# Context weights stored 32 bytes further on in their tiles, in a two-layer mixer block on one core

## The chip, the cores and the metric

The kernel runs on one core of a Trainium2 chip. The metric is the device time of one execution in microseconds (us). TensorE (PE) does the matrix products and loads their weights (PEld in the profile), ScalarE (ACT) the activations, VectorE (DVE) elementwise work, GpSimd (POOL) a few powers, SyncE (SP) issues the transfers.

## The reference

A stream `x` of 512 tokens and a context of 256 tokens, both 1024 wide, go through two layers. In each, both are normalised and modulated, projected by one wide matrix, and mixed by four branches (retention, a short convolution, a 31-tap convolution, windowed attention); each branch is gated, and an output matrix brings the sum back. The second layer needs of the context only keys and values.

```
for l in range(DEPTH):                       # 2
    hx = modulate(rmsnorm(x, norm_w[l]), shift_x, scale_x)
    hc = modulate(rmsnorm(xc, norm_w[l]), shift_c, scale_c)
    px = split_proj(hx @ w_in[l])
    pc = split_proj(hc @ w_in[l])            # layer 1: ret_k, ret_v, att_k, att_v alone
    ...
    # mixer_output, for x and (in layer 0) for the context:
    merged = sum(sigmoid(g) * (br @ w_branch[i]) for i, (g, br) in enumerate(zip(gates, (r, s, f, a))))
    out = merged @ w_out
    x = x + gate_x * out_x
    xc = xc + gate_c * out_c
return rmsnorm(x, final_norm_w)
```

## The kernel before

Everything is held transposed, with 128 channels on the partitions and the tokens along the columns: 512 columns for the stream, 256 for the context. A weight of a projection (kind "a"), gate ("g") or output ("o") is a block of 1024 input channels by 128 output channels, held as [128, 1024], that is eight chunks of 128 x 128 side by side, 512 bytes each in a partition.

To keep float32 accuracy every operand is split into a high part and a low part, each of a type (float32r) that TensorE takes in one pass. `split` and `pair` do it for the data, `w_split` for the weights: ACT copies the raw weight into the high tile `wh`, DVE subtracts and writes the low tile `wl`. `mm3` then makes three products for each chunk: high weight x high data, high weight x low data, low weight x high data. So a weight has 8 x 3 = 24 products, all added up in one of three PSUM tiles `d`. For the context the high and low data of a chunk (256 columns each) lie in one row of 2048 bytes, one behind the other (`pair`, `Half`); for the stream each has a row of its own.

The weight tiles are three pairs (`self.wt`, `wh0`, `wl0`, `wh1`, ...), taken in turn by `take`. They are allocated one behind the other in one pool, and behind them lie the softmax tiles `p`, the constants `cst`, `vec` and small tables. A weight's key is (kind, layer, index, s), with s = 1 for the context and 0 for the stream; so `key[3]` is s. For s = 1 the raw weight comes in two rows of 512 columns and is split in two halves (208 in all), for s = 0 in one tile of 1024 columns. For kind "g" a second weight, that of the branch, is split into two rows (`wkeep`) and not into `wt`.

TensorE's order is that of the program. `w_get` hands out a weight and lets `w_ahead` split the next ones until two are ready. Beside the dense products run side flows (attention, retention, convolution taps, norms), which `slot` puts between the products by estimates of a planner (`Tally`).

The order of the run: `start` makes the context's norm and its first three projections chunk by chunk; its modulation products there use `s4`, a weight tile of 4 columns read at `s4[:, 2 * h + k]`, with h from 0 to 3 and k 0 or 1, four floats (16 bytes) apart. Then come the context's mixer (54 projections in all, 32 gates) and `mix_out` (8 outputs), the stream's mixer of layer 0, ten key and value projections of the context for layer 1, the stream's mixer of layer 1, and `final`, which makes the stream's last output in two halves of 256 columns.

Of the kernel before, what the change touches and what calls it, by code (L numbers as in the profile page):

```python
# [9 lines left out]
F32R = mybir.dt.float32r  # L10
# [15 lines left out]
P = 128  # L26
# [97 lines left out]
class Row:  # L124
# [3 lines left out]
    def __init__(self, free, ring, tile, w, parts):  # L128
        self.free, self.ring = free, ring
        self.r = tile[:, :w] if parts else None  # L130
        self.a = tile[:, :w].bitcast(F32) if parts else tile[:, :w]
# [146 lines left out]
class Block:  # L278
    def __init__(self, ctx, tc, xc, vec, cst, w_a, w_g, w_b, w_o, w_m, out):
        self.tc, self.nc = tc, Tally(tc.nc)  # L280
        self.xc, self.out = xc, out
        self.wsrc = {"a": w_a, "g": w_g, "b": w_b, "o": w_o}
        self.w_m = w_m

        rp = ctx.enter_context(tc.tile_pool(name="rp", bufs=1))
        rp.tile([P, PAD], F32, name="fill")
        self.arena = Arena(rp, NROWS, 12)
        self.arena.relief = self.relief

        self.cp = cp = ctx.enter_context(tc.tile_pool(name="cp", bufs=1))  # L290
        self.wraw = [cp.tile([P, 1024], F32, name=f"w{i}") for i in range(2)]
        self.wt = [[cp.tile([P, 1024], F32R, name=f"w{p}{i}") for p in "hl"] for i in range(3)]
        self.pt = [cp.tile([P, 640], F32, name=f"p{i}") for i in range(6)]
        pp = ctx.enter_context(tc.tile_pool(name="pp", bufs=1, space=PSUM))
        nc = self.nc
        self.cst = cp.tile([P, NC_], F32, name="cst")
        self.vec = cp.tile([P, NV], F32, name="vec")
        nc.sync.dma_start(self.vec, vec)
        nc.sync.dma_start(self.cst[:, :NCE], cst[:, :NCE])
        self.late_consts = lambda: nc.sync.dma_start(self.cst[:, NCE:], cst[:, NCE:])  # L300
        self.rings = {}
        self.dense = [pp.tile([P, 512], F32, name=f"d{i}") for i in range(3)]
        self.ovs = [pp.tile([P, 512], F32, name="ov")]
        self.work = [pp.tile([P, 512], F32, name=f"k{i}") for i in range(4)]
        self.turn = {}
        self.wq, self.wraws, self.wready, self.wkeep = [], [], {}, {}
        self.lanes = [[] for _ in range(5)]
        self.turns = 0
        self.flow = None
# [135 lines left out]
    def w_split(self):  # L445
        nc = self.nc
        key, raws = self.wraws.pop(0)
        parts = [self.take("wt")]
        for _, raw, o in raws:
            if o is None:  # L450
                hi, lo = self.part(), self.part()
                self.wkeep[key] = (hi, lo)
                hi, lo = hi.r, lo.r
                parts.append((hi, lo))
            else:
                hi, lo = (x[:, o] for x in parts[0])
            nc.scalar.activation(hi, raw, AF.Copy)
            nc.vector.tensor_tensor(lo, raw, hi.bitcast(F32), op=ALU.subtract)
        self.wready[key] = parts
# [1011 lines left out]
```

## Time and profile before

| | |
|---|---|
| median of 3 runs | 1831.67 us (1830.37 to 1833.78) |
| the profiled execution | 1832.62 us, of which the span from its first to its last instruction is 1830.5 us |
| mean granted clock of TensorE | 0.994 |
| PE, PEld, DVE, ACT busy | 98%, 85%, 73%, 46% of the span |

A time in the profile is that of one profiled execution. PE's busy time holds the recorded durations of matmuls, which overlap one another; how fast PE goes is seen from the distance between two starts (the pitch). A granted clock of 1.00 is 2.4 GHz.

### The profile page before, as it was taken

What the parts mean: (1) busy time and instruction counts of PE and PEld (TensorE: products, weight loads), DVE (VectorE), ACT (ScalarE), POOL (GpSimd) and SP (SyncE); (2) the same over time, 40 slices, a digit from 0 to 9 for tenths busy, and PEclk for the clock granted to TensorE, in tenths of its full rate; (3) what the DMA queues carried; (4) which work ended last, traced back from release to release, by engine and by line L of the source; (5) the groups of instructions that cost most, each with busy time, mean ns of one, the idle gap of its engine ahead of it and who ended that gap; (6) DMA issues with size and microseconds to landing.
All of it is one profiled execution on the core that took longest, in us unless ns stands there. A gap on an engine that the chain in (4) does not pass through costs nothing. (4 is left out here: it accounts for less than half of the span.)

```text
span 1830.5 us, 27546 instructions
## 1 busy us (share of the span) xinstructions
PE 1799.5 (98%) x10224; PEld 1562.1 (85%) x10224; DVE 1329.4 (73%) x2643; ACT 847.1 (46%) x1616; POOL 27.9 (2%) x34
## 2 busy tenths in 40 slices
PE   6999999999999999999999999999999999999997
PEld 4999999998888888788888889888888888888887
DVE  8899999884556669996898457447999865444445
ACT  6666765553554544423423336445534554323232
POOL 1000000000000000000000000000000000000000
PEclk8999999999999999999999999999999999999999
DMA  8736377743122222233555552322122222332233
GB/s 306 252 125 213 111 242 231 235 138 116 69 70 67 84 81 83 91 108 124 185 170 168 169 182 75 116 70 70 66 91 87 80 98 87 115 104 87 87 117 114
DMA packets 104646, 232.60 MB, mean 127 GB/s; under 512 B 12864, under 2 KB 20800, under 8 KB 104512
## 3 DMA queue, kind: packets, MB, share of 16 engines
q1 hardware_dynamic: 104512, 230.84, 37.9%
q8 instruction: 80, 1.31, 0.3%
q14 instruction: 54, 0.44, 0.1%
HBM read 218.73 MB, written 5.24 MB: 122 GB/s over the span
## 5 line engine op out<-in xcount | busy, mean ns | idle before, releaser
L187 PE MATMUL d<-r,wh 128*128 128x512 f32 (+1 forms) x3136 | 942.7, 383 | 0.3 <-DVE r L187 0.3
L187 PEld LDWEIGHTS d<-r,wh 128*128 128x128 f32 x3136 | 572.7, 188 | 106.2 <-DVE r L187 0.5
L187 PE MATMUL d<-r,wl 128*128 128x512 f32 (+1 forms) x1568 | 597.6, 381 | 0.0
L187 DVE TENSOR_TENSOR wl<-w,wh 128x1024 fp32r<-128x1024 f32 x193 | 235.6, 1221 | 233.8 <-ACT wh L187 229.0
L187 ACT ACTIVATE wh<-w 128x1024 fp32r<-128x1024 f32 x193 | 205.0, 1062 | 411.5 <-PE d L187 358.2
L187 PEld LDWEIGHTS d<-r,wl 128*128 128x128 f32 x1568 | 294.8, 188 | 57.6
L187 ACT ACTIVATE r<-r 128x512 fp32r<-128x512 f32 (+3 forms) x264 | 150.5, 588 | 211.6 <-DVE r L187 94.5
L187 DVE TENSOR_TENSOR r<-r,r 128x512 fp32r<-128x512 f32 (+5 forms) x338 | 207.8, 629 | 35.2 <-ACT r L187 31.2
L187 DVE SCALAR_TENSOR_TENSOR r<-r,h_cfw,r 128x503 f32<-128x503 f32 (+19 forms) x360 | 229.1, 648 | 2.0
L187 PE MATMUL d<-r,r 128*128 128x512 f32 x768 | 184.8, 389 | 0.5 <-DVE r L187 0.5
L187 ACT ACTIVATE wh<-r 128x512 fp32r<-128x512 f32 x208 | 129.2, 631 | 101.7 <-PE d L187 88.5
L187 PEld LDWEIGHTS d<-r,r 128*128 128x128 f32 x768 | 144.1, 188 | 30.8 <-DVE r L187 0.9
L187 DVE TENSOR_TENSOR wl<-r,wh 128x512 fp32r<-128x512 f32 x208 | 140.6, 685 | 18.6 <-ACT wh L187 17.5
L187 DVE SCALAR_TENSOR_TENSOR r<-r,d 128x512 f32<-128x512 f32 (+1 forms) x156 | 92.7, 594 | 56.4 <-PE d L187 32.4
L187 ACT ACTIVATE r<-d 128x512 f32<-128x512 f32 (+2 forms) x234 | 118.5, 507 | 14.1 <-PE d L187 9.5
L187 PE MATMUL k<-r,r 128*128 128x128 f32 (+2 forms) x752 | 112.3, 290 | 2.7 <-ACT p L187 2.6
L187 ACT ACTIVATE r<-k 128x512 fp32r<-128x512 f32 (+4 forms) x162 | 76.9, 522 | 70.5 <-PE k L187 69.2
L187 PEld LDWEIGHTS k<-r,r 128*128 128x128 f32 x752 | 99.5, 191 | 8.9 <-ACT p L187 6.2
L187 ACT ACTIVATE p<-k,s_nm 128x256 f32<-128x256 f32 (+1 forms) x144 | 69.7, 497 | 78.0 <-DVE s_nm L187 77.9
L187 DVE SCALAR_TENSOR_TENSOR r<-r,cs,r 128x256 f32<-128x256 f32 x196 | 83.6, 477 | 2.0 <-DMA r<-w_m 1.4
L187 DVE TENSOR_TENSOR r<-k,r 128x512 fp32r<-128x512 f32 (+2 forms) x88 | 54.4, 651 | 9.5 <-ACT r L187 9.3
L187 ACT ACTIVATE p<-p,s_rc 128x512 f32<-128x512 f32 (+2 forms) x80 | 51.3, 719 | 9.6 <-DVE s_rc L187 9.6
(393 smaller groups left out, 2245.3 us busy)
## 6 DMA issues: line engine op xcount, KB each, us to landing
w<-w_a SPq DMA_DIRECT2D x108, 512.0 KB, 3.5
r<-w_a SPq DMA_DIRECT2D x128, 256.0 KB, 5.0
w<-w_g SPq DMA_DIRECT2D x64, 512.0 KB, 3.5
r<-w_m SPq DMA_DIRECT2D x96, 256.0 KB, 3.8
r<-w_b SPq DMA_DIRECT2D x96, 256.0 KB, 3.4
r<-w_g SPq DMA_DIRECT2D x64, 256.0 KB, 3.8
w<-w_o SPq DMA_DIRECT2D x21, 512.0 KB, 3.5
r<-xc SPq DMA_DIRECT2D x24, 256.0 KB, 3.8
```

Source lines behind the costliest of these rows:

```text
L187: return f(*a, **k)
```

## The change

The six weight tiles get 1040 columns in place of 1024. `w_split` uses, of each tile that it takes, the 1024 columns from column 8 x `key[3]` on: from column 8 (32 bytes) for a weight of the context, from column 0 for one of the stream. The slices that it writes are also those that it hands to the products. Nothing else changes.

```
-        self.wt = [[cp.tile([P, 1024], F32R, name=f"w{p}{i}") for p in "hl"] for i in range(3)]
+        self.wt = [[cp.tile([P, 1040], F32R, name=f"w{p}{i}") for p in "hl"] for i in range(3)]
...
         key, raws = self.wraws.pop(0)
-        parts = [self.take("wt")]
+
+        parts = [[x[:, 8 * key[3]:8 * key[3] + 1024] for x in self.take("wt")]]
```

## Rows read from the trace of the kernel before

**Rows 1.** The page's first part: busy time of an engine, its share of the span, its instructions.
```profile
PE 1799.5 (98%) x10224; PEld 1562.1 (85%) x10224; DVE 1329.4 (73%) x2643; ACT 847.1 (46%) x1616; POOL 27.9 (2%) x34
```

**Rows 2.** Busy time by stretch, in the context's mixer: the stretch in us, its length, busy us and instructions of each engine, granted clock of PE, share of the DMA engines, GB/s.
```profile
core 0: us, PE busy (x) PEld busy (x) DVE busy (x) ACT busy (x) POOL busy (x), PEclk, DMA share, GB/s
...
90.00:135.00 45.00, 45.00 (x381) 45.00 (x381) 42.92 (x105) 27.47 (x67) 0.86 (x1) 1.00 0.38 124
135.00:180.00 45.00, 45.00 (x376) 44.60 (x375) 43.79 (x120) 30.47 (x73) 3.23 (x3) 1.00 0.62 202
180.00:225.00 45.00, 45.00 (x376) 44.83 (x375) 44.85 (x109) 32.06 (x79) 0.00 (x0) 1.00 0.40 127
225.00:270.00 45.00, 45.00 (x376) 44.83 (x375) 40.84 (x90) 28.17 (x58) 1.17 (x2) 1.00 0.69 227
270.00:315.00 45.00, 45.00 (x378) 45.00 (x378) 42.34 (x98) 23.76 (x48) 0.00 (x0) 1.00 0.76 243
315.00:360.00 45.00, 45.00 (x379) 45.00 (x378) 39.33 (x86) 25.21 (x52) 0.19 (x1) 1.00 0.79 253
```

**Rows 3.** Groups of PE's matmuls with 256 columns, different tiles and shapes apart, over the whole run: output, moving tile, weight tile, shapes, count, busy us and mean ns of one, idle time before. First the two groups of `final`, then the first and the last of 24 forms of the context's layer 0 mixer, the first and the last of 24 of layer 1's keys and values, and two of the 24 of `mix_out`.
```profile
L187 PE MATMUL d<-r,wh 128*128 128x256 f32 x256 | 46.7, 284 | 0.3 <-DVE r L187 0.3
...
L187 PE MATMUL d<-r,wl 128*128 128x256 f32 x128 | 36.2, 283 | 0.0
...
L187 PE MATMUL d<-r51h,wh 128*128 128x256 f32 x86 | 26.5, 309 | 0.2 <-ACT r L187 0.2
...
L187 PE MATMUL d<-r51l,wh 128*128 128x256 f32 x86 | 24.3, 282 | 0.0
...
L187 PE MATMUL d<-r1166h,wh 128*128 128x256 f32 x10 | 3.5, 346 | 0.0
...
L187 PE MATMUL d<-r1166h,wl 128*128 128x256 f32 x10 | 2.8, 282 | 0.0
L187 PE MATMUL d<-r580h,wh 128*128 128x256 f32 x8 | 2.7, 333 | 0.0
...
L187 PE MATMUL d<-r617h,wh 128*128 128x256 f32 x8 | 2.3, 283 | 0.0
```

**Rows 4.** PE's timeline in the context's mixer, the first and the last of eleven matmuls in a row: start us, duration us, what it is.
```profile
200.01 0.28 PE L187 MATMUL d<-r81h,wl 128*128 128x256 f32 x1
...
201.21 0.28 PE L187 MATMUL d<-r133h,wh 128*128 128x256 f32 x1
```

**Rows 5.** The chain of work that ended last, in order of time: the longest piece, the stream's gates in layer 1 (start us, length us, what, how many).
```profile
1526.90 244.83 PE d L187 x1080
```

**Rows 6.** One tile's instructions, weight loads and matmuls: shortest, median and longest duration in ns, first and last start in us. First the low weights of the stream (512 columns, and 256 in `final`), then a form of the context, then the stream's gate branches, whose weights lie in rows.
```profile
L187 PEld LDWEIGHTS d<-r,wl x1568: 187/188/192, 393.1 to 1818.8; 128*128 128x128 f32 x196
L187 PE MATMUL d<-r,wl x1568: 278/389/398, 393.3 to 1819.0; 128*128 128x512 f32 x180, 128*128 128x256 f32 x16
...
L187 PEld LDWEIGHTS d<-r51h,wl x86: 187/192/192, 31.8 to 363.9; 128*128 128x128 f32 x86
L187 PE MATMUL d<-r51h,wl x86: 278/283/288, 31.9 to 364.0; 128*128 128x256 f32 x86
...
L187 PE MATMUL d<-r,r x768: 388/389/498, 778.3 to 1771.3; 128*128 128x512 f32 x192
```

**Rows 7.** The same view for the products with the 4-column weight tile `s4` (256 columns, in `start`; some of them ran at the lower clock).
```profile
L187 PEld LDWEIGHTS k<-r,s x128: 82/84/128, 7.0 to 46.6; 128*4 128x4 f32 x128
L187 PE MATMUL k<-r,s x128: 276/279/774, 7.0 to 46.8; 128*4 128x256 f32 x128
```

**Rows 8.** The page's costliest groups: the two instructions that write half a context weight.
```profile
L187 ACT ACTIVATE wh<-r 128x512 fp32r<-128x512 f32 x208 | 129.2, 631 | 101.7 <-PE d L187 88.5
...
L187 DVE TENSOR_TENSOR wl<-r,wh 128x512 fp32r<-128x512 f32 x208 | 140.6, 685 | 18.6 <-ACT wh L187 17.5
```

**Rows 9.** Groups of DVE by shape from 40 to 404 us: taps of the context's convolution; a tap that is n columns shorter than 256 reads or writes from column n on.
```profile
L187 DVE SCALAR_TENSOR_TENSOR r<-r,h_cfw,r 128x255 f32<-128x255 f32 x8 | 3.8, 476 | 0.0
L187 DVE SCALAR_TENSOR_TENSOR r<-r,h_cfw,r 128x254 f32<-128x254 f32 x8 | 3.8, 475 | 0.0
L187 DVE SCALAR_TENSOR_TENSOR r<-r,h_cfw,r 128x253 f32<-128x253 f32 x8 | 3.8, 475 | 0.0
L187 DVE SCALAR_TENSOR_TENSOR r<-r,h_cfw,r 128x252 f32<-128x252 f32 x8 | 3.8, 474 | 0.0
...
L187 DVE SCALAR_TENSOR_TENSOR r<-r,h_cfw,r 128x241 f32<-128x241 f32 x8 | 3.6, 463 | 0.0
```

**Rows 10.** Groups of PE's matmuls with 512 columns and weights from `wt`, over the whole run.
```profile
L187 PE MATMUL d<-r,wh 128*128 128x512 f32 x2880 | 896.0, 392 | 0.0
L187 PE MATMUL d<-r,wl 128*128 128x512 f32 x1440 | 561.3, 390 | 0.0
```

**Rows 11.** Waits of PE over the whole run, two of ten lines: who waited for whom, us in total, times, longest us.
```profile
PE k L187 <- DVE r L187: 8.0, 6, 2.2
...
PE d L187 <- DVE wl L187: 0.6, 1, 0.6
```

**Rows 12.** Waits of all engines from 45 to 375 us, one line.
```profile
ACT wh L187 <- PE d L187: 72.9, 91, 2.0
```

## The prediction

> **What bounds the kernel now.** I read the page's first part before anything else: TensorE (PE) is busy for 98% of the span, and weight loads (PEld), VectorE (DVE) and ScalarE (ACT) for 85%, 73% and 46% [rows 1]. The clock was full and PE without a gap in every stretch of 45 us from 90 to 360 us, the context's mixer, in which nearly all of the touched products lie; the thing to see there is that DVE is nearly as full, between 39.3 and 44.9 us of each 45 [rows 2]. So the end is set by how far apart PE starts its matmuls, if DVE keeps up.
>
> The second thing is how many products the edit reaches. A form of the context's 24 products per weight stands 86 times (54 projection weights and 32 gate weights), one of the output's 8 times, one of the second block's key and value products 10 times [rows 3]. Each weight has 8 chunks in three products, so each kind has 24 forms: 24 x (86 + 8 + 10) = 2496 matmuls. The gate branch's own products, whose weights lie in rows (`wkeep`), and the 256 + 128 products of `final` (256 columns, but the stream's, so shifted by 0) [rows 3] are not among them.
>
> The third is the pitch, start to start. In the context ten matmuls in a row start 1.20 us after one another: 120 ns each [rows 4]. In the stream's products of 512 columns 1080 take 244.83 us: 226.7 ns [rows 5]. At 2.4 GHz, the level that a granted clock of 1.00 is [rows 2], 256 and 512 columns are 106.7 and 213.3 ns, so either pitch is 13.3 ns longer than its columns. These 13.3 ns are all that the edit can win in a product.
>
> The fourth is whether they are fixed. A matmul's recorded time is its pitch plus about 163 ns: 283 at 120 [rows 4], 389 at 226.7 [rows 5, 6]. So the minimum, median and maximum of a group give the pitches that occur. One form of the context's products has 278, 283 and 288, that is 115, 120 and 125 ns, and the weight loads of the same form take 187 to 192 ns, most of them 192 [rows 6]. The products of 512 columns go up to 398 (235 ns) with loads of mostly 188 [rows 6]. The same work on the same tiles at a full clock thus costs up to 10 ns more or less, and the load, which runs beside the matmul before it, stretches with it. I read that as the two reads of PE getting in each other's way, by an amount that depends on how they lie against each other in time. In the context the pair has settled where the load is at its longest.
>
> **The change part by part.**
>
> *The shift by 32 bytes.* `w_split` writes both halves of a context weight 8 floats further on and PE reads them from there. It adds no instruction, wait or transfer; the order on all queues (SP's, which loads the raw weights, and POOL's among them) stays. What may change is the relation of the weight read to the moving read, which still starts on its row. No row shows a full weight load at another offset within 512 bytes, so its cost is bounded from both sides. From below: the products with a 4-column weight tile (`s4`), also of 256 columns, have a minimum of 276 ns, a pitch of 113 [rows 7]; 7 ns less than 120, times 2496, is 16.6 us (2496 x 6.67). From above: 288 ns, a pitch of 125 [rows 6], 2496 x 5 = 12.5 us more. I take 117 ns, about the middle of 113 and 120, because the present state has the longest load of those recorded, so that most displacements that do anything lead to a shorter one: 2496 x 3 = 7.5 us less.
>
> *What speaks against it.* The weight tile of those 4-column products is read at eight starts 16 bytes apart (`s4[:, 2h + k]`), and the median over all of them, 279 ns, lies 3 ns above the minimum [rows 7]: a start that is off by 16 to 112 bytes does nothing visible to a load of 4 columns. The Trainium skill goes further. TensorE: Matmul & The Clock Gate, Step-by-step: what each phase is for, says that TensorE has two independent read ports and that loading the next weights takes no read bandwidth from the running matmul; by that rule the place of a weight is of no account and the time stays. The trace doesn't bear the rule out fully: load and matmul stretch together [rows 6].
>
> *ScalarE's and VectorE's writes.* ACT writes the halves of `wh` (208 at 631 ns) and DVE those of `wl` (208 at 685 ns) 32 bytes later [rows 8]. The conv taps show that DVE doesn't mind an offset: they start 4 to 60 bytes into a row, and with one column less each they take 476, 475, 475 and 474 ns [rows 9]. I count nothing. For ACT no row has such an offset; it is idle for a third of these stretches [rows 2], so even a few per cent on 631 ns would be hidden.
>
> *The longer tiles.* Each of the six tiles grows by 64 bytes, so the second to sixth move by 64 to 320 bytes, and all behind them (softmax tiles, constants) by 384. The stream's 4320 products of 512 columns [rows 10] then read weights that lie up to 320 bytes off their old place. One ns on each would be 4.3 us. The bounds are again recorded ones: from above 398 ns, a pitch of 235, +8.3 ns or 36 us; from below 388 ns in the group that holds 512-column products alone, -1 ns or 4.3 us [rows 6]. I take 0, since these products sit at a median of 389 with a load that is not stretched (188) [rows 6], and because a whole multiple of 64 bytes changes less of how two reads lie than half of 64 does.
>
> *What becomes late next.* A faster PE asks for weights sooner. PE waited for a `wl` once in the whole run, for 0.6 us, while ACT stood idle before `wh` for 72.9 us in 91 waits on PE between 45 and 375 us [rows 11, 12]: the splits are ahead of PE and wait for it to give tiles back. From 135 to 225 us DVE works 43.8 + 44.9 = 88.6 us of 90 [rows 2]; at 117 ns this stretch would last 87.8 us and DVE would be 0.9 us short, which one weight ready ahead (24 x 0.12 = 2.9 us) covers. At 113 ns, 90 to 225 us would take 127.5 us against 131.6 us of DVE work [rows 2]: 4 us short, about what the lead holds, so up to 2 us of the 16.6 may be lost there. Without that cover every missing DVE us would be a PE us.
>
> **The sum.** The profiled execution took 1832.6 us (span 1830.5). 1832.6 - 7.5 = 1825.1. It lies 0.95 us above the median of the runs shown (1831.7), so on the median's footing 1824.2.
>
> **The rivals.**
>
> *Nothing moves.* The pitch is set by something that doesn't know addresses (the exchange of weights itself): the same 13.3 ns at 256 and at 512 columns speaks for it, also the 16-byte steps of the small tile [rows 4, 5, 7]; the spread of 278 to 288 at one and the same place speaks against it [rows 6]. 1831.7 us. SBUF — State Buffer of the Trainium skill, SBUF: two separate sides, sides with this rival ("PE, ACT, and DVE's dedicated pair never wait on anyone"). Chance 0.24.
>
> *A worse lock.* The shift puts the two reads into the relation that is now met for single matmuls only: 288 ns or 125 [rows 6]. Place: every one of the 2496 products, nothing hides it, because PE has no gap. +12.5 us, 1844; at +2 ns, 1837. It decides from a pitch of 121.5 (+3.7 us). A weight column block that no longer begins where its 512 bytes begin would work the same way. Chance 0.16.
>
> *The other products move more than those meant.* The 512-column products leave their 226.7 ns because of the 64-byte steps. +2 ns is 4320 x 2 = 8.6 us, 1833 with the forecast's gain, 1840 without. Their present 389 ns is near the minimum of 388 and far from the 398 [rows 6], so I hold a loss for likelier. Chance 0.06 slower, 0.03 faster.
>
> *The gain is whole.* The context's pitch goes to 113 as in the 4-column products: 1815, or 1817 with DVE's shortage. It is the far end of the forecast's own case.
>
> The edit surely does what it says: writer and reader take the same slices.
>
> **How the numbers follow.** Forecast with its far end (pitch 113 to 118.5) 0.51, nothing 0.24, a worse lock 0.16, the other products 0.09. A measurement of this kernel tells about 0.2% (3.7 us) from no change. Faster by more than that: 0.51 + 0.03 = 0.54; within: 0.24; slower: 0.16 + 0.06 = 0.22. The likeliest case alone reaches from 1815 to 1828. The range goes from 1813 (the whole gain and a little from the 512-column products) to 1840 (a pitch of 123.5 in the context, or 2 ns on the others without a gain); left out are the worst locks and a loss on both kinds, about 1 in 10.
>
> **What would show it.** Right: the context's 256-column products at 275 to 281 ns in place of 283, loads shorter than 192, the mixer's stretch some 7 us shorter, 512-column products at 389 as now, `final` at 283 as now. Wrong: 283 and 192 unchanged (nothing moves); 285 or more (a worse lock); 389 moved (the other products); the context's matmuls shorter, but new waits of PE on `wl`, or DVE full in all stretches (DVE took the gain).

## The result, and the profile after

The changed kernel takes 1845.41 us (median of 6 runs, 1843.92 to 1846.84), the kernel before 1831.56 us in the same measurement (6 runs, 1830.37 to 1833.78). The ratio is 1.0075, with a 95% interval from 1.0062 to 1.0088: slower by 13.9 us. The forecast was 1824.2 us, with a range from 1813 to 1840. The profiled execution has a span of 1842.3 us.

On the page of the changed kernel the engines' instruction counts are those of [rows 1]. PE's busy time grew by 13.0 us, DVE's and ACT's stayed within 0.7 us, and that of the weight loads became shorter by 4.5 us:

```profile
PE 1812.5 (98%) x10224; PEld 1557.6 (85%) x10224; DVE 1330.1 (72%) x2643; ACT 846.6 (46%) x1616; POOL 27.9 (2%) x34
```

The view of one tile's instructions shows best where the time went (shortest, median and longest ns, then first and last start; compare [rows 6]). Low weights of the stream, then one form of the context, then the branch products, whose weights lie in rows:

```profile
L187 PEld LDWEIGHTS d<-r,wl x1568: 187/188/192, 389.5 to 1830.6; 128*128 128x128 f32 x196
L187 PE MATMUL d<-r,wl x1568: 277/397/400, 389.7 to 1830.7; 128*128 128x512 f32 x180, 128*128 128x256 f32 x16
...
L187 PEld LDWEIGHTS d<-r51h,wl x86: 187/188/193, 30.8 to 360.4; 128*128 128x128 f32 x86
L187 PE MATMUL d<-r51h,wl x86: 277/281/285, 31.0 to 360.5; 128*128 128x256 f32 x86
```
```profile
L187 PE MATMUL d<-r,r x768: 387/389/500, 778.6 to 1784.0; 128*128 128x512 f32 x192
```

Read the starts first. The stream's first product with a low weight comes at 389.7 us in place of 393.3: the context's part, the one the change is about, became 3.6 us shorter. From there to the last product with a low weight it is 1441.0 us, and it was 1425.7: the stream's part, in which all weights but the ten of the context's second layer keep column 0, became 15.3 us longer. The medians say the same of single products: the context's 283 became 281, with loads that are no longer stretched (188 for 192), and the stream's 389 became 397, near the longest that the trace of before had (398). The branch products, whose weights are not in the changed tiles, keep a median of 389.

Groups by shape over the whole run give the total (busy us, mean ns). First the two that [rows 10] show, then `final`'s, which answer to the first lines of [rows 3]:

```profile
L187 PE MATMUL d<-r,wh 128*128 128x512 f32 x2880 | 905.1, 395 | 0.0
L187 PE MATMUL d<-r,wl 128*128 128x512 f32 x1440 | 569.6, 396 | 0.0
L187 PE MATMUL d<-r,wh 128*128 128x256 f32 x256 | 45.8, 282 | 0.3 <-DVE r L187 0.3
L187 PE MATMUL d<-r,wl 128*128 128x256 f32 x128 | 35.9, 280 | 0.0
```

The 512-column groups went from 392 to 395 and from 390 to 396 ns: 2880 x 3 + 1440 x 6 = 17.3 us. `final`'s 256-column products, not meant by the change either, became shorter.

The chain that ended last has the same longest piece as before, now 248.96 / 1080 = 230.5 ns a product where it was 226.7 [rows 5]:

```profile
1535.43 248.96 PE d L187 x1080
```

No other kind of work moved by more than about 1 us. The clock stays at 1.00 in the context's mixer (busy time by stretch, columns as in [rows 2]), and of PE's waits the one on `wl` [rows 11] is still a single one:

```profile
135.00:180.00 45.00, 45.00 (x379) 44.61 (x378) 44.10 (x120) 30.21 (x73) 3.23 (x3) 1.00 0.63 213
180.00:225.00 45.00, 44.94 (x377) 44.50 (x376) 44.85 (x107) 32.39 (x81) 0.00 (x0) 1.00 0.36 111
```
```profile
PE d L187 <- DVE wl L187: 0.8, 1, 0.8
```

**Mean pitches.** A median hides products that take two or three values in turn, so below I also use means of the pitch, worked out from the starts of all matmuls in a trace: the start of the next less the own start, for two neighbours with the same number of columns, without gaps longer than the columns at 2.4 GHz plus 30 ns (of the kernel before that keeps 4161 of the 4320 products of 512 columns with weights from `wt`, and 2424 of the context's 2496). Before: 227.39 ns at 512 columns, 119.85 in the context, 119.90 in `final`, 226.67 for the branch products. After: 231.60, 118.46, 117.45, 228.00. So 4320 x 4.21 = +18.2 us, 2496 x (-1.39) = -3.5, 384 x (-2.45) = -0.9, 768 x 1.33 = +1.0: +14.8 us (+14.7 with the context's own branch products, whose pitch fell by 0.25 ns), where 13.9 was measured. Summed over all starts, with the products that this mean leaves out, the four kinds took +16.6, -3.2, -0.9 and +1.0 us, together +13.5; the two profiled executions differ by 11.8, since all other work was 1.7 us shorter. So the pitch of TensorE's products explains the change within about 2 us.

### The profile page after: what moved, and what is told of

It is laid out like the page before. It is cut to its first block, busy times and chain, and to the rows that moved or that the text cites. A ratio compares the mean times of both kernels' runs of the same rounds, so it can differ in the third digit from the quotient of the medians.

```text
span 1842.3 us, 27546 instructions
## 1 busy us (share of the span) xinstructions
PE 1812.5 (98%) x10224; PEld 1557.6 (85%) x10224; DVE 1330.1 (72%) x2643; ACT 846.6 (46%) x1616; POOL 27.9 (2%) x34
## 5 line engine op out<-in xcount | busy, mean ns | idle before, releaser
L187 PE MATMUL d<-r,wl 128*128 128x512 f32 (+1 forms) x1568 | 605.5, 386 | 0.0
L187 DVE SCALAR_TENSOR_TENSOR r<-r,h_cfw,r 128x503 f32<-128x503 f32 (+19 forms) x360 | 229.3, 648 | 2.0
L187 ACT ACTIVATE r<-d 128x512 f32<-128x512 f32 (+2 forms) x234 | 118.6, 507 | 14.8 <-PE d L187 10.2
```

The source lines that it names most:

```text
L187: return f(*a, **k)
```

## The experiments

**The theory.** What sets the pitch is where a weight chunk begins against the rows of the moving data, counted within a few hundred bytes; I call this its place. In the kernel before, every weight of `wt` has place 0. In the changed kernel 1040 columns are 4160 bytes, 64 more than a multiple of 512, so the stream's six tiles have places 0, 64, 128, 192, 256 and 320, and the context's are these plus 32. The rivals: what counts is not the place but that the two tiles of a pair, used in turn, differ from one another; or the absolute address; or the shift itself does harm. In the texts on record A1 is the theory, A2 that a loss needs two tiles that differ. Some versions give the three pairs of tiles names of their own (a, b, c), so that the trace tells them apart.

**One part alone: longer tiles, no shift** (names by letter, nothing else).

```
-        self.wt = [[cp.tile([P, 1024], F32R, name=f"w{p}{i}") for p in "hl"] for i in range(3)]
+        self.wt = [[cp.tile([P, 1040], F32R, name=f"w{p}{i}") for p in "hl"] for i in "abc"]
```

> The tiles get 1040 columns, but nothing is shifted: the second to sixth tile move by 64 to 320 bytes, and a context weight begins where its tile begins. (The tiles are named by letters, so that the profile keeps the three pairs apart.) Theory A (the loss comes from the 64-byte steps between the tiles, the 32 bytes as such are a gain or nothing): the stream's 512-column products are as slow as with the change, medians of 392 to 397 ns for some tiles in place of 389, and the time is 1842 to 1850 us. Rival B (the shift by 32 bytes makes the loss): 389 ns in every tile, 1828 to 1834 us. By A, wha, which did not move, should still be the best or near it, and the context's 256-column products should stand below 283 ns, since their weights have left the old place too.

**The other part alone: the shift, in tiles that keep their places** (1152 columns are 9 x 512 bytes).

```
-        self.wt = [[cp.tile([P, 1024], F32R, name=f"w{p}{i}") for p in "hl"] for i in range(3)]
+        self.wt = [[cp.tile([P, 1152], F32R, name=f"w{p}{i}") for p in "hl"] for i in "abc"]
...
-        parts = [self.take("wt")]
+        parts = [[x[:, 8 * key[3]:8 * key[3] + 1024] for x in self.take("wt")]]
```

> The shift by 32 bytes alone: the tiles get 1152 columns, so each begins a whole multiple of 512 bytes behind the other, as before, and only the context's weights lie 32 bytes further on. Theory A: the stream's products are back at 389 ns, the context's stay near the 281 ns that the changed kernel shows, 1 to 2.5 ns less each, and 2496 of them make 1825 to 1829 us. Rival B: the context's products are slow here (285 or more) and the time is 1840 or more. Rival C (the place of a weight does nothing to the context, its 2 ns come from somewhere else): 283 ns and 1831 us.

**The same with 128 bytes** (32 in place of both 8s).

> As the run before, with 128 bytes in place of 32. In the changed kernel the pair of high-weight products of 256 columns in final, whose second tile pair lies 128 bytes off, came 114 ns after one another. If a pitch is a function of the offset within 512 bytes, all of the context's products should be near 114 to 118 ns (277 to 281 ns recorded): 1815 to 1827 us, and at the low end DVE should be full and PE wait for weights. If those 114 ns were a passing state: 283 ns, 1831 us.

**Another absolute address** (data rows and weights move together by 64 bytes, places stay).

```
-PAD = 480
+PAD = 496
```

> The kernel before with a filler tile 64 bytes longer, ahead of everything: data rows and weight tiles all move by 64 bytes together. If what counts is where the weight read lies relative to the moving read: no change, 389 and 283 ns, 1828 to 1834 us. If it is the place itself (a read that begins 64 bytes into a block of 512): the 512-column products should be slower as with the change, 1840 us or more.

Measured against 1830.85 us (25 runs of before on the same chip):

| version | median us | ratio, 95% interval | 512 columns, ns | context, ns |
|---|---|---|---|---|
| longer tiles alone | 1842.59 (4 runs) | 1.0061, 1.0046 to 1.0076 | 231.61 | 117.39 |
| shift by 32 alone | 1827.59 (10 runs) | 0.9980, 0.9971 to 0.9990 | 227.38 | 118.24 |
| shift by 128 alone | 1828.37 (10 runs) | 0.9985, 0.9975 to 0.9994 | 227.36 | 118.76 |
| all moved by 64 together | 1831.75 (10 runs) | 1.0003, 0.9994 to 1.0012 | 227.37 | 119.86 |

The longer tiles alone slow the stream's products as much as the whole change does (231.61 ns, 231.60), and the shift alone is a gain. The longest piece of the chain, with the longer tiles alone, with the shift alone, and with all moved together:

```profile
1534.88 248.96 PE d L187 x1080
```
```profile
1521.76 244.83 PE d L187 x1080
```
```profile
1527.17 244.83 PE d L187 x1080
```

The last of these says that a move of 64 bytes which takes everything along is of no account. The shift alone, seen at one form of the context (loads, matmuls), has unstretched loads and 281 ns for 283. Its six tiles lie alike, so a pitch can change without tiles that differ:

```profile
L187 PEld LDWEIGHTS d<-r51h,wla x29: 187/188/192, 30.4 to 355.6; 128*128 128x128 f32 x29
L187 PE MATMUL d<-r51h,wla x29: 278/281/288, 30.5 to 355.7; 128*128 128x256 f32 x29
```

The two parts don't simply add up (+11.7 and -3.3 us, together 13.9). With longer tiles alone the context's weights, too, have places from 0 to 320, and their pitch is already 117.39: -6.1 us. The shift takes them to 118.46 from there, a loss of 2.7 us. What the shift does depends on the place it starts from. The text on 128 bytes expected 114 to 118 ns and 1815 to 1827 us; it missed on both, with 118.76 ns and 1828.37 us.

The same traces bear on two further points. The edit also moves where ScalarE and VectorE write the weights, and that could be what counts; but with the longer tiles alone the stream's products have 231.5 ns while a write of `wh` or `wl` runs beside them and 231.7 while none does (1087 and 3074 products, from the starts). Pairs a (places 0 and 64) and c (256 and 320) have the same pitches there, 229.3 ns with the high weight and 234.4 and 234.8 with the low one, as if 256 bytes were no displacement.

**Scans of places.** Tiles of 1152 columns, and each pair of tiles read at a column of its own (four bytes each). Each ran once.

```
-        parts = [self.take("wt")]
+        offs = (((16, 16), (32, 32), (8, 8)), ((32, 48), (16, 16), (48, 32)))[key[3]][self.turn.get("wt", 0) % 3]
+        parts = [[x[:, o:o + 1024] for x, o in zip(self.take("wt"), offs)]]
```

> A scan for what sets the pitch. Each of the three tile pairs (a, b, c) begins at a multiple of 512 bytes, and the weights of each lie at offsets of their own (high, low tile, in bytes). Stream: a 64 and 64, b 128 and 128, c 32 and 32. Context: a 128 and 192, b 64 and 64, c 192 and 128. Theory A1 (the place of a weight read relative to the moving read sets the pitch, whether or not the tiles of a pair differ): the stream's products leave 389 ns in at least two of the three pairs, by 3 ns or more. Theory A2 (a loss needs two tiles that differ by 64 bytes in their offset): all three pairs stay at 389 ns, and only the context's a and c differ from b. For the context, by the run with the long tiles, a should be at 116 to 117 ns a product, recorded as 279 to 280; b at 118.

The second, columns of the high and the low tile of pairs a, b and c: stream (4, 4), (64, 64), (0, 32), context (32, 64), (64, 64), (48, 48).

> The same scan with other offsets. Stream: a 16 and 16, b 256 and 256, c 0 and 128. Context: a 128 and 256, b 256 and 256, c 192 and 192. By A1 the stream's a is off 389 ns by less than its b or c if the effect grows with the distance, and all three are off it; by A2 only c is. For the context no number is expected beyond 112 to 122 ns a product; the pair with the lowest is the one for a kernel that uses one place for all.

The third: stream (48, 48), (40, 40), (56, 56), context (48, 48), (44, 44), (52, 52).

> A scan, not a version: tiles of 1152 columns; the stream's pairs a, b, c at 192, 160 and 224 bytes, the context's at 192, 176 and 208 bytes. If the effect has a period of 256 bytes and is even about 0, then 192 is like 64 (512 columns: 233 ns) and 224 like 32 (233 ns); if it is not even, some of the three lie below 227.3 ns. For 256 columns: 192 gave 114.6 ns, 176 and 208 within 1 ns of it if the best place is broad, at 117 or more if it is a point. Time about 1831 + 4320 x 5 ns - 2496 x 4 ns = 1843 if all three of the stream's places are bad.

They took 1848.61, 1836.65 and 1846.74 us (before: 1832.51 for the first two, 1832.32 for the third). Products of one pair tell a place's pitch. The stream's low weights in the first scan, places 64, 128 and 32, the high weight of a pair at the same place as the low one; all three are slow, so A2 falls:

```profile
L187 PE MATMUL d<-r,wla x520: 276/394/398, 400.3 to 1829.3; 128*128 128x512 f32 x160, 128*128 128x256 f32 x14
L187 PE MATMUL d<-r,wlb x528: 274/393/404, 389.2 to 1832.1; 128*128 128x512 f32 x163, 128*128 128x256 f32 x13
L187 PE MATMUL d<-r,wlc x520: 276/395/401, 394.7 to 1835.0; 128*128 128x512 f32 x158, 128*128 128x256 f32 x16
```

and in the second, groups by shape, places 256, 16, and low at 128 with high at 0:

```profile
L187 PE MATMUL d<-r,wlb 128*128 128x512 f32 x488 | 190.4, 390 | 0.0
L187 PE MATMUL d<-r,wla 128*128 128x512 f32 x480 | 188.6, 393 | 0.0
L187 PE MATMUL d<-r,wlc 128*128 128x512 f32 x472 | 187.2, 397 | 0.0
```

At 256 the 390 ns of before are back, against A1's text, which expected all three pairs off it; at 16 it is 393. One form of the context in the second scan, with places 256 (`wlb`) and 192 (`wlc`):

```profile
L187 PE MATMUL d<-r51h,wlb x29: 278/283/415, 31.7 to 360.1; 128*128 128x256 f32 x29
...
L187 PE MATMUL d<-r51h,wlc x28: 276/276/415, 32.3 to 350.8; 128*128 128x256 f32 x28
```

Mean pitches from the starts, for two neighbours with weights from `wt`, high and low weight at the same place (in brackets: the place used by that pair alone, between pairs at others):

| place, bytes | 0 | 16 | 32 | 64 | 128 | 160 | 176 | 192 | 208 | 224 | 256 |
|---|---|---|---|---|---|---|---|---|---|---|---|
| 512 columns, ns | 227.4 | (231.1) | (233.1) | (233.3) | (232.4) | (233.3) | | (229.6) | | (233.2) | (227.8) |
| context, 256 columns, ns | 119.85 | | 118.2 | 116.45 (115.3) | 118.8 | | (118.2) | 116.8 (114.6, 116.3) | (116.8) | | (119.8) |

The two rows run against each other: places 0 and 256 are the best for 512 columns and the worst for 256. Both come back after 256 bytes. The third scan's guess that the curve is even about 0 held for 224 (233.2, like 32) and failed for 192 (229.6, where 64 has 233.3). The first scan's text expected 118 ns of the context at 64; it was 115.3. `final`, whose 256-column products use the stream's places, has 119.8 ns at 160 in the third scan, so 0 and 256 are not the only bad places for 256 columns. No run has the whole stream at one place other than 0.

**A better version: the stream at 0, the context at 192.** (The second of these three moves the weights of the last output, too.)

```
-        parts = [self.take("wt")]
+        parts = [[x[:, 48 * key[3]:48 * key[3] + 1024] for x in self.take("wt")]]
```

> Weight tiles of 1152 columns (each a whole multiple of 512 bytes behind the other), context weights 48 columns (192 bytes) into their tiles, stream weights at column 0. Theory (the offset of the weight's read to the moving data's, modulo 256 bytes, sets the pitch): the run with pairs at several offsets had 114.6 ns at 192 bytes against 119.9 at 0, so 2496 products x 5.3 ns = 13 us less, 1831 - 13 = 1818; products of 512 columns stay at 227.3 ns. First rival (VectorE then becomes the bound in the context's mixer, since from 135 to 225 us it already worked 88.6 us of 90): 1820 to 1824, with waits of PE on wl. Second rival (the offset had worked only because the pairs of tiles differed from one another): 1831, pitch 120.

```
+        o = 48 if key[3] or key[:2] == ("o", DEPTH - 1) else 0
+        parts = [[x[:, o:o + 1024] for x in self.take("wt")]]
```

> As the run with the context's weights at 192 bytes, and the weights of the stream's last output (final, 384 products of 256 columns) at 192 bytes too. Theory: what counts is the number of columns (256) and the offset, not whose weight it is: a further 384 x 5.3 ns = 2 us less, 1816, and final's products at 278 ns in place of 283. Rival (the gain hangs on the context's layout, with high and low data in one row): final's products stay at 283 and the time is that of the run before it within 0.5 us.

**The context at 64** (16 in place of both 48s of the first).

> As the run with the context's weights at 192 bytes, but at 64 bytes: all three pairs alike, the stream at 0. In the first scan pair b at 64 bytes, between two other pairs, had 115.3 ns; at 192 bytes a pair between two others had 114.6, but with all three pairs at 192 the mean was 116.8 and the time 8 us under before. Theory A (the place of a weight alone sets its pitch): 115.3 again, 2496 x 4.6 ns = 11 us less than before, 1820. Theory B (the state that the products before leave behind counts as well, so that a row of equal pairs settles elsewhere than a pair that stands between others): not 115.3, more likely 116 to 118, 5 to 9 us less than before, 1823 to 1827.

| version | median us | before | ratio, 95% interval | context, ns | `final`, ns |
|---|---|---|---|---|---|
| context at 192 | 1824.38 (5 runs) | 1832.32 (9) | 0.9962, 0.9949 to 0.9974 | 116.76 | 119.89 |
| context and `final` at 192 | 1825.72 (5 runs) | 1832.32 (9) | 0.9962, 0.9948 to 0.9975 | 116.85 | 117.77 |
| context at 64 | 1824.99 (6 runs) | 1831.14 (10) | 0.9968, 0.9955 to 0.9980 | 116.45 | 119.88 |

All three are faster than the kernel before by 6 to 8 us, and none reached the 11 to 15 us that the texts had for a fixed pitch at each place. The timeline shows why: a chain of products at one and the same place has more than one pitch. With the context at 192, nine products of one weight take 1.06 us, 118 ns each, and eight microseconds later, behind products of another kind, ten of another take 1.13 us, 113 ns each (start us, duration us, what):

```profile
202.26 0.28 PE L187 MATMUL d<-r51l,whb 128*128 128x256 f32 x1
...
203.32 0.28 PE L187 MATMUL d<-r95l,whb 128*128 128x256 f32 x1
```
```profile
208.71 1.12 PE L187 MATMUL k<-r,r 128*128 128x256 f32 x8
...
210.12 0.28 PE L187 MATMUL d<-r67l,wha 128*128 128x256 f32 x1
...
211.25 0.28 PE L187 MATMUL d<-r109h,wla 128*128 128x256 f32 x1
```

What went before a stretch of products has a part, next to the place, in the pitch on which it settles. The trace at 192 has 59 stretches of 14 or more context products with nothing between them (pitch from the second start on): 19 run at 113 ns and 38 at 118, and only 2 lie higher, at 123 and 125. All 3 that follow products `k<-r,r` of 256 columns are at 113, and all 20 that follow `k<-cst,p` or `k<-cst,r` are at 118; behind the context's branch products it is 15 and 8. At 64 it is the other way round: the 23 stretches behind branch products are all at 118, and 10 of the 14 behind `k<-cst,p` and `k<-cst,r` of 128 columns are at 113 to 114. That is Theory B of the last text, and 116.45 ns at 64 bytes, where 115.3 stood between other pairs, bears it out. `final` at 192 gained 2.1 ns, so the number of columns counts and not whose weight it is; 384 x 2.1 = 0.8 us is too little to be seen in the time.

Of the rival of VectorE as the bound there is only a trace. No wait of PE on `wl` was added, but eight transposes of softmax tiles between the products took 1.73 and 1.95 us, where they took 1.03 and 1.04 before, 1.6 us more (PE's timeline, with the context at 192, then before). Over the whole run such transposes took only 0.5 us more (from the starts):

```profile
200.57 1.73 PE L187 MATMUL k<-cst,p 128*128 128x128 f32 x8
...
218.06 1.95 PE L187 MATMUL k<-cst,p 128*128 128x128 f32 x8
```
```profile
204.81 1.03 PE L187 MATMUL k<-cst,p 128*128 128x128 f32 x8
...
221.94 1.04 PE L187 MATMUL k<-cst,p 128*128 128x128 f32 x8
```

**The sum, for all versions.** Mean pitches less those of before, times 4320 (512 columns), 2496 (context), 384 (`final`) and 768 (branch products), against the difference of the medians, in us: changed kernel +14.7 and +13.9; longer tiles +12.0 and +11.7; shift by 32 -4.4 and -3.3; by 128 -2.9 and -2.5; all moved -0.1 and +0.9; scans +15.3 and +16.1, +5.3 and +4.1, +13.0 and +14.4; context at 192 -7.8 and -7.9; with `final` -8.5 and -6.6; at 64 -8.6 and -6.2. (These sums also hold some tenths for the context's branch products.) Eleven kernels agree within 2.5 us. For the larger changes the pitch leaves little else to explain; for the last two the sum has about 2 us that the medians do not show.

## Why the prediction was wrong

**The step that failed** is "The longer tiles", with "I take 0". The stream's 4320 products were priced at nothing "because a whole multiple of 64 bytes changes less of how two reads lie than half of 64 does". No row stood behind that sentence, and the scans contradict it: 64 bytes cost 5.9 ns (233.3 less 227.4), 32 bytes 5.7, 16 bytes 3.7; only 256 bring the old value back. Measured, the term is +4.2 ns or 18.2 us. The bounds it was given, -4.3 and +36 us, held; their middle, about +16 us, would have been near. The other reason named, that the products "sit at a median of 389 with a load that is not stretched", was read the wrong way round. The context was said to gain because its products sat in a bad relation, from which most displacements lead to a better one. By the same reading the stream's products sat at the good end of 388 to 398 [rows 6], from which most displacements lead to a worse one. The text says so in the rival "The other products move more than those meant", but gives it 6 in 100 and 2 ns; its sign, "389 moved (the other products)", is what the trace shows.

**The shift by 32 bytes** was right in kind and too large. Alone it took 1.6 ns and 4.0 us by the pitches, 3.3 us by the measured times, where 3 ns and 7.5 us were forecast. In the changed kernel the context has 1.4 ns less. The bounds of 113 and 125 ns held for the context's mean at every place tried.

**What speaks against it.** The rivals "Nothing moves" and "A worse lock" fell: the context has 118.24 ns, and less than 119.85 at every place tried for it but 0 and 256. The Trainium skill (TensorE: Matmul & The Clock Gate, Step-by-step: what each phase is for) says that loading the next weights takes no read bandwidth from the running matmul. The prediction drew from it that the place of a weight is of no account. Moving the weights against the data changed the pitch of the same 4320 products by 4 ns, and moving both together changed nothing, so that conclusion is wrong here; whether read bandwidth is what is lost, no run shows. SBUF — State Buffer of the Trainium skill, SBUF: two separate sides, says that PE never waits on anyone; the runs show a pitch that depends on the place, but not what brings it about.

**ScalarE's and VectorE's writes** cost nothing, as forecast: the busy time of DVE and ACT is that of [rows 1] within 0.7 us.

**What becomes late next** held: no new wait on `wl`, at up to 3.4 ns less a product; what came late, by 1.6 us in the context's mixer, were two rows of softmax transposes, which had not been named.

**The range** ended at 1840, 5.4 us too low, because it took 2 ns as the loss of the other products and left out a larger one.

**What stays open.** That two reads of PE hinder each other would explain that the place against the data counts, but no run shows the reads. The last product with a branch weight, which lies at 0, has 226.7 ns when the next weight lies at 0, 225.8 at 64 and 226.0 at 192, but 235.0 at 32 and 236.8 at 160 (17 or 18 products each, worked out from the starts with the longer tiles alone and of the scans). So the place of the next weight, whose load runs beside the product, counts already by itself; yet a chain at 64 or 192 does not stay at 226. How a chain finds its pitch was not settled. All else in SBUF moved together with the data in the run that moved both, so that it is the data of the same product against which a place counts is the simplest reading, not one that a run isolates.

## What to carry to other kernels

An edit of a tile's size moves all that is allocated behind it: list every product whose operands move, by its count, before pricing the few that are meant. Where a recorded duration of one and the same product varies, ask at which end of its spread the present state sits; from the good end a displacement loses, and it should be priced at the middle of the spread, not at nothing. To move one operand alone, grow the tile by a length that keeps the others' places (here a multiple of 512 bytes): the same shift of the context's weights then gained 3.3 us, and one of 192 bytes 7.9.

## What the runs showed of the hardware

- The pitch of matmuls with a weight load between each two depends on where the weight begins against the moving data, and comes back after 256 bytes: 227.4 ns at 0 and 227.8 at 256 for 512 columns, 231.1 to 233.3 at 16 to 160 bytes, 229.6 at 192; moving both together by 64 bytes changes nothing (227.37, 119.86).
- The best place differs with the number of columns: 0 for 512 columns; for 256 columns 0 is among the worst (119.85), with 256 and, in `final`, 160 (119.8), and 64 and 192 are the best tried (116.45 and 116.76 in a version, 114.6 between other pairs).
- At one place a chain can run at different pitches for a while: 113 and 118 ns eight microseconds apart with the context at 192, where 57 of 59 stretches run at one or the other. Which it is goes in part with the work that came before.
